# A decoder trunk whose second token half lags one block of rows at each change of sublayer

## The chip, the cores and the metric

The kernel runs on one core of a Trainium2 chip. The metric is the device time of one execution in microseconds, as a median over runs. All matrix work is TensorE's (PE in the profile; PEld is its weight load), ScalarE is ACT, VectorE is DVE, GpSimd is POOL, and SyncE (SP) issues nearly all DMA transfers, in program order.

## The reference, cut to what matters

A trunk of two layers over 256 tokens of width 1024. Layer 0 is FFN, gated short convolution, FFN. Then the keys and values are built once, and layer 1 is FFN, sparse attention, FFN. Every sublayer is wrapped in the same two steps, with shift, scale and gate taken from the condition `c`:

```python
h = modulate_pre(x, g[s, 0], mod[:, s, 0], mod[:, s, 1])   # rms_norm(x) * (1 + scale) + shift
y = sublayer(h)
x = gated_post_add(x, y, g[s, 1], mod[:, s, 2], weight)    # x + weight * gate * rms_norm(y)
...
def swiglu_ffn(h, w_in, w_out):                            # hidden width 2816
    g, u = jnp.split(h @ w_in, 2, axis=-1)
    return (jax.nn.silu(g) * u) @ w_out
```

`mod` is `silu(c) @ ada_w + ada_b`: 18 vectors of 1024, and two more for the keys and values. Attention has 16 heads in 4 groups and three branches (compressed blocks, selected blocks, window), each a masked softmax with linear position penalties, merged by sigmoid gates. With 256 tokens all blocks are selected, so the selected and the window branch are two causal softmaxes with keys and values of their own. All data are float32.

## The kernel before, in words

**Products.** Each float32 product is made of three matmuls in the type fp32r (`mm3`): high part of the activations with high and low part of the weights, low part with high part. The weights are streamed: a DMA brings 1 MB into one of three buffers `raw`, and each half of it, a *unit*, is split into `whi` (ScalarE, a copy that rounds) and `wlo` (VectorE, a subtraction). `fwd(n, g)` splits the next `n` units of a fixed list (`w_init`), and beside them makes `g` adaLN steps. Units lie in two pools, A with room for six and B for four; the list says which. A `raw` buffer takes its next load when both its halves are split (`w_dma`).

**adaLN steps.** One step (`g_step`, line 204) multiplies a 128 x 1024 piece of `ada_w` by the condition and adds along the row, on VectorE. There are 160; 16 are made at the start, the others are strewn among the weight splits by `pump` at the rates `G_FFN`, `G_CONV`, `G_KV` and `G_ATT`. `g_need` makes those still missing when a vector is used.

**Tokens in two halves.** The 256 tokens are two halves of 128 (`t`). An FFN has 11 blocks of 256 hidden columns. For block `b` the kernel makes the input product of half 0 and of half 1 (24 matmuls each), gates and transposes the result to `H[b]`, and adds the rows of the output weights of the block before, `wo(b - 1)`, to the accumulators `y[0]` and `y[1]` (12 matmuls each). All engines' orders are written out by hand.

**A change of sublayer** (`turn_over`) finishes `y[0]`, then `y[1]` with the last two blocks (24 matmuls each), while ScalarE, GpSimd and VectorE take the mean square of `y[0]`, update `x` for half 0, take its mean square and scale it (`normed`). Then TensorE transposes half 0, ScalarE and VectorE modulate and split it into `hx` (`h_split`, lines 354 to 364), and the next sublayer's first product follows. Half 1 goes the same way one step later. The function `first` of the next sublayer gives four pieces of its work, which `turn_over` puts between its own.

**Attention.** `q_first` gives the first query product and the compression: `compress` multiplies 128-row blocks by four unsplit weight pieces `w1` of 1 MB, two for the keys and two for the values, which go through the same `raw` buffers (`w_whole`). `nsa` makes the rest of the queries, the gates (`gates`, weights `bg`) and the compressed keys and values. `heads` is a loop over 16 heads. In iteration `i` it transposes the weights of head `i` (`trans`), scales those of head `i + 1` (`soft_b`, lines 935 to 939), makes minimum and exponential for head `i + 3` (`soft_a`, lines 927 and 928), and issues the scores of head `i + 4`; every second iteration multiplies two heads by the values (`pv`). The compressed branch's scores are turned into exponentials by `cmp_soft` and normalised by the function that it returns (`cmp_norm`, called `fin`), and `cmp_trans` transposes them for `pv`.

**Start.** The condition is loaded into 128 partitions at once and passed through Silu; `x` is normed and transposed; then eight rounds of two adaLN steps, the modulation of one column block and eight matmuls in float32 give the first two blocks of the first FFN.

## Time and profile before

| | |
|---|---|
| median of 3 runs (lowest to highest) | 1077.45 us (1074.9 to 1077.48) |
| the profiled execution: time, span | 1074.75 us, 1073.0 us |
| busy in the span: PE, PEld | 1034.8 us, 829.0 us |
| busy in the span: DVE, ACT, POOL | 776.7 us, 530.5 us, 29.4 us |
| mean granted clock of TensorE | 0.992 of full speed |
| moved by DMA | 263.51 MB, mean 246 GB/s |

Busy time of an engine is the time in which one of its instructions ran. TensorE's matmuls overlap and their ends are modelled, so a busy TensorE need not be at its peak, and the granted clock of a stretch is read beside it. The span runs from the first to the last instruction; 1.75 us of the execution's time lie around it. The profile is of a single execution.

### The profile page before, as it was taken

To read this page: it belongs to the slowest core of one execution; us is meant where nothing else is said; L and a number is where in the kernel's file an instruction comes from. 1 tells how busy PE (TensorE), PEld (TensorE's weight loads), DVE (VectorE), ACT (ScalarE), POOL (GpSimd) and SP (SyncE) were. 2 spreads that over 40 slices of the span, in tenths; PEclk is the share of its full clock that TensorE was granted. 3 is DMA by queue.
4 is the path that set the end of the run, shared out by engine and by line. 5 is a ranking of instruction groups with operands and counts; after the bars stand their busy time and mean duration, and the time that the engine had idled before them with its cause. 6 is when DMAs were issued, how large, how long until landed. Compare 5 with 4: busy or idle time off the path is not lost. (4 is left out here: it accounts for less than half of the span.)

```text
span 1073.0 us, 13377 instructions
## 1 busy us (share of the span) xinstructions
PE 1034.8 (96%) x4862; PEld 829.0 (77%) x4862; DVE 776.7 (72%) x1348; ACT 530.5 (49%) x974; POOL 29.4 (3%) x84
## 2 busy tenths in 40 slices
PE   5999999999999999999999999999989899999997
PEld 3478888878878888887988888886877668888886
DVE  4678878878866788788777787785558675666453
ACT  3344444566555444346664344455378664444342
POOL 0000000010010000001100000001000010000000
PEclk9999999999999999999999999999989999999999
DMA  9978888936836898886647988895411355554541
GB/s 364 415 290 304 324 325 313 354 137 249 301 118 223 301 319 323 324 316 252 233 165 279 341 318 322 310 336 204 189 40 41 119 200 211 197 216 161 196 153 40
DMA packets 51090, 263.51 MB, mean 246 GB/s; under 512 B 5584, under 2 KB 8016, under 8 KB 30288
## 3 DMA queue, kind: packets, MB, share of 16 engines
q1 hardware_dynamic: 50640, 261.61, 66.6%
q0 software_dynamic: 384, 1.05, 0.4%
q8 instruction: 38, 0.62, 0.2%
q14 instruction: 28, 0.23, 0.1%
HBM read 260.54 MB, written 1.05 MB: 244 GB/s over the span
## 5 line engine op out<-in xcount | busy, mean ns | idle before, releaser
L248 PE MATMUL in<-whiA,hx 128*128 128x512 f32 x776 | 305.6, 394 | 3.5 <-ACT hx L355 1.8
L250 PE MATMUL in<-whiA,hx 128*128 128x512 f32 x776 | 304.8, 393 | 0.0
L249 PE MATMUL in<-wloA,hx 128*128 128x512 f32 x776 | 303.3, 391 | 0.8 <-DVE wloA L151 0.8
L151 DVE TENSOR_TENSOR wloA<-raw,whiA 128x1024 fp32r<-128x1024 f32 (+1 forms) x209 | 250.4, 1218 | 48.6 <-ACT whiA L145 48.6
L145 ACT ACTIVATE whiA<-raw 128x1024 fp32r<-128x1024 f32 (+1 forms) x209 | 210.3, 1052 | 13.1 <-DMA raw<-in_wi_dram 4.6
L204 DVE SCALAR_TENSOR_TENSOR graw<-graw,sc 128x1024 f32<-128x1024 f32 x147 | 178.8, 1218 | 0.6 <-DMA graw<-in_ada_dram 0.6
L250 PEld LDWEIGHTS in<-whiA,hx 128*128 128x128 f32 x776 | 146.0, 188 | 35.3 <-DVE hx L358 4.9
L248 PEld LDWEIGHTS in<-whiA,hx 128*128 128x128 f32 x776 | 146.0, 188 | 35.0 <-ACT hx L355 2.8
L418 ACT ACTIVATE sg<-in 128x256 f32<-128x256 f32 x86 | 33.1, 385 | 277.4 <-PE in L250 277.4
L249 PEld LDWEIGHTS in<-wloA,hx 128*128 128x128 f32 x776 | 146.2, 188 | 31.0 <-DVE wloA L151 1.4
L248 PE MATMUL y<-whiB,H 128*128 128x512 f32 x368 | 150.6, 409 | 0.0
L249 PE MATMUL y<-wloB,H 128*128 128x512 f32 x368 | 144.3, 392 | 2.1 <-DVE wloB L151 2.1
L250 PE MATMUL y<-whiB,H 128*128 128x512 f32 x368 | 144.6, 393 | 0.9 <-DVE H L292 0.9
L151 DVE TENSOR_TENSOR wloB<-raw,whiB 128x1024 fp32r<-128x1024 f32 x108 | 129.4, 1221 | 13.8 <-ACT whiB L145 13.8
L419 DVE TENSOR_TENSOR ht<-in,sg 128x256 f32<-128x256 f32 x86 | 36.4, 424 | 115.9 <-ACT sg L418 115.8
L145 ACT ACTIVATE whiB<-raw 128x1024 fp32r<-128x1024 f32 x108 | 108.5, 1054 | 4.6 <-PE in L249 2.8
L250 PEld LDWEIGHTS y<-whiB,H 128*128 128x128 f32 x368 | 69.1, 188 | 16.5 <-DVE H L292 1.6
L249 PEld LDWEIGHTS y<-wloB,H 128*128 128x128 f32 x368 | 69.4, 189 | 15.7 <-DVE wloB L151 3.3
L248 PEld LDWEIGHTS y<-whiB,H 128*128 128x128 f32 x368 | 69.2, 188 | 12.0
L291 ACT ACTIVATE H<-tr 128x256 fp32r<-128x256 f32 x88 | 33.1, 382 | 80.0 <-PE tr L286 80.0
L292 DVE TENSOR_TENSOR H<-tr,H 128x256 fp32r<-128x256 f32 x88 | 36.5, 420 | 28.2 <-ACT H L291 28.2
L286 PE MATMUL tr<-sm,ht 128*128 128x128 f32 x192 | 35.7, 272 | 0.7 <-DVE H L292 0.7
(209 smaller groups left out, 974.9 us busy)
## 6 DMA issues: line engine op xcount, KB each, us to landing
raw<-in_wi_dram SPq DMA_DIRECT2D x84, 1024.0 KB, 6.7
graw<-in_ada_dram SPq DMA_DIRECT2D x147, 512.0 KB, 5.5
raw<-in_wo_dram SPq DMA_DIRECT2D x44, 1024.0 KB, 6.8
raw<-in_cv_dram SPq DMA_DIRECT2D x12, 1024.0 KB, 6.5
whiB<-in_ada_dram SPq DMA_DIRECT2D x8, 512.0 KB, 9.5
raw<-in_ao_dram SPq DMA_DIRECT2D x4, 1024.0 KB, 6.2
raw<-in_q_dram SPq DMA_DIRECT2D x4, 1024.0 KB, 5.4
raw<-in_w_dram SPq DMA_DIRECT2D x4, 1024.0 KB, 7.7
```

The costliest lines, as they stand in the source:

```text
L145: nc.scalar.activation(hi[:, :w], raw, AF.Copy)
L151: nc.vector.tensor_sub(lo, raw, hi.bitcast(F32))
L204: self.nc.vector.scalar_tensor_tensor(w, w, 1.0, self.sc, op0=OP.mult, op1=OP.mult, accum_out=self.mod[:, m, k:k + 1])
L248: mm(out, xh, wh, start=start, stop=False, skip_group_check=True)
L249: mm(out, xh, wl, start=False, stop=False, skip_group_check=True)
L250: mm(out, xl, wh, start=False, stop=stop, skip_group_check=True)
L286: self.nc.tensor.transpose(o[:, i * 128:i * 128 + 128], src[:, i * 128:i * 128 + 128], self.ident)
L291: self.nc.scalar.activation(h[0], src, AF.Copy)
L292: self.nc.vector.tensor_sub(h[1], src, h[0].bitcast(F32))
L418: nc.scalar.activation(sg, o[:, 0:256], AF.Silu)
L419: nc.vector.tensor_mul(ht, o[:, 256:512], sg)
```

## The change

- **Lag.** At the end of an FFN the rows of block 8 are added to `y[0]` in their old place, but to `y[1]` only in the change of sublayer, ahead of blocks 9 and 10 (`late`). After the convolution and attention one row block of eight does the same. The rows of block 10 go to pool A.
- **Rates.** No adaLN steps in the first block of the first FFN and in the last block of each; other rates are changed to match. `turn_over` splits 2 + 2 units in place of 1 + 2, and 2 + 4 in place of 1 + 4 ahead of the keys.
- **Attention.** Three units (the gates' and the first query pair's) are split behind the compression and the second query product, not before them. In the loop the splits of iterations 0, 1, 2 and 12 go, those of 13 and 14 come. The compressed branch's second softmax starts at iteration 5, not 6, and the normalisation stands behind `soft_b` of iterations 1 and 6. Two more units are split before the change to the last FFN.
- **Condition.** `c` is loaded into one partition, two matmuls with a row of ones spread it over 128, and Silu reads the result from PSUM.

```diff
-    G_FFN = (1.5, 1.5, 1.5, 0.45)
-    G_CONV = 0.75
+    G_FFN = (1.65, 1.65, 1.6, 0.45)
+    G_CONV = 1.25
     G_KV = 1.25
-    G_ATT = 1.5
+    G_ATT = 1.0
...
-            p.append((a["wo"][n, b], [("wo", n, b, i) for i in range(2)], "B", 1024))
+            p.append((a["wo"][n, b], [("wo", n, b, i) for i in range(2)], "A" if b == 10 else "B", 1024))
...
-    def turn_over(self, rows, ma, mb, first, mid=None, more=(1, 2)):
+    def turn_over(self, rows, late, ma, mb, first, mid=None, more=(2, 2)):
...
         self.prod_out(0, rows, False, True, each0)
-        self.prod_out(1, rows, False, True, each1)
+        self.prod_out(1, late + rows, False, True, each1)
...
-        g = self.G_FFN[n]
+        rate = self.G_FFN[n]
...
             last = b == 10
+            g = 0 if last or first is not None else rate
...
             if last:
-                self.fwd(3)
-                return nxt(self.rows(n, 9) + self.rows(n, 10), lambda: self.turn_in(h1, H, 1)())
+                self.fwd(2)
+                return nxt(self.rows(n, 9) + self.rows(n, 10), self.rows(n, 8), lambda: self.turn_in(h1, H, 1)())
...
             for i, q in enumerate(wait):
-                self.prod_out(1, self.rows(n, q), new and i == 0, False)
-                Hs.pop(q)
+                if q < 8:
+                    self.prod_out(1, self.rows(n, q), new and i == 0, False)
+                    Hs.pop(q)
...
-        self.prod_out(1, rows(0, 4), True, False)
+        self.prod_out(1, rows(0, 3), True, False)
         self.fwd(2)
-        return nxt(rows(4, 8), None)
+        return nxt(rows(4, 8), rows(3, 4), None)
...
             if i + 1 < NH:
                 soft_b(i + 1)
+            if i in (1, 6):
+                fin()
             if i + 3 < NH:
                 soft_a(i + 3)
...
-            if i in (0, 6):
-                fin = self.cmp_soft(i // 6)
+            if i in (0, 5):
+                fin = self.cmp_soft(i // 5)
             if i + 4 < NH:
                 bias(i + 4)
-            if i in (0, 7):
-                fin()
...
-            if i < 4 or i in (12, 14):
-                self.fwd(1)
+            if i in (3, 13, 14):
+                self.fwd(2 if i == 14 else 1)
...
         o = self.prod(("q0",), 1)
+        self.fwd(3)
         self.then()
...
         self.fwd(4, g)
-        self.prod_out(1, rows(0, 4), True, False)
-        self.fwd(2, 2 * g)
-        return nxt(rows(4, 8), None)
+        self.prod_out(1, rows(0, 3), True, False)
+        self.fwd(4, 2 * g)
+        return nxt(rows(4, 8), rows(3, 4), None)
...
-        nc.sync.dma_start(self.sc, bass.AP(tensor=cc.tensor, offset=cc.offset, ap=[[0, 128], [1, D]]))
+        cr = self.quarter()[0:1, :]
+        nc.sync.dma_start(cr, bass.AP(tensor=cc.tensor, offset=cc.offset, ap=[[0, 1], [1, D]]))
...
-        nc.scalar.activation(self.sc, self.sc, AF.Silu)
+        ones = self.tmp.tile([128, 256], F32, name="sg")[0:1, 0:128]
+        nc.vector.memset(ones, 1.0)
+        for h in range(2):
+            o = self.bank("tr")
+            sl = slice(h * 512, h * 512 + 512)
+            nc.tensor.matmul(o, ones, cr[:, sl], start=True, stop=True)
+            nc.scalar.activation(self.sc[:, sl], o, AF.Silu)
```

VectorE in the first block of the first FFN, before (L151 is the low half of a weight split, L204 an adaLN step, L292 the low half of `H`):

```order
L292 TENSOR_TENSOR H<-tr,H 128x2x128 x4
L151 TENSOR_TENSOR wloA<-raw,whiA 128x1024
L204 SCALAR_TENSOR_TENSOR graw,mod<-graw,sc 128x1024
L151 TENSOR_TENSOR wloA<-raw,whiA 128x1024
L419 TENSOR_TENSOR ht<-in,sg 128x256
L151 TENSOR_TENSOR wloB<-raw,whiB 128x1024
L204 SCALAR_TENSOR_TENSOR graw,mod<-graw,sc 128x1024
L151 TENSOR_TENSOR wloB<-raw,whiB 128x1024 x2
L204 SCALAR_TENSOR_TENSOR graw,mod<-graw,sc 128x1024
```

The same place in the changed kernel:

```order
L292 TENSOR_TENSOR H<-tr,H 128x2x128 x4
L151 TENSOR_TENSOR wloA<-raw,whiA 128x1024 x2
L419 TENSOR_TENSOR ht<-in,sg 128x256
L151 TENSOR_TENSOR wloB<-raw,whiB 128x1024 x4
L419 TENSOR_TENSOR ht<-in,sg 128x256
L292 TENSOR_TENSOR H<-tr,H 128x2x128
L151 TENSOR_TENSOR wloA<-raw,whiA 128x1024
L292 TENSOR_TENSOR H<-tr,H 128x2x128
L151 TENSOR_TENSOR wloA<-raw,whiA 128x1024 x2
L204 SCALAR_TENSOR_TENSOR graw,mod<-graw,sc 128x1024
```

The three adaLN steps that stood between these splits are gone from here; the first step now comes behind nine splits.

SyncE around the compression, before (the 2048-wide loads from `in_w` are the four pieces `w1`; `bg` are the gates' weights):

```order
L130 DMA raw<-in_bg_dram 128x384
L194 DMA graw<-in_ada_dram 128x1024
L130 DMA raw<-in_w_dram 128x2048 x3
L765 DMA cst<-in_cst_dram 128x778
L767 DMA w_6175<-in_w_dram 128x384
L130 DMA raw<-in_w_dram 128x2048
L130 DMA raw<-in_q_dram 128x2048
```

The same place in the changed kernel:

```order
L130 DMA raw<-in_bg_dram 128x384
L130 DMA raw<-in_w_dram 128x2048 x2
L767 DMA cst<-in_cst_dram 128x778
L769 DMA w_6177<-in_w_dram 128x384
L130 DMA raw<-in_w_dram 128x2048 x2
L130 DMA raw<-in_q_dram 128x2048
```

The third piece `w1` has moved from ahead of the constants to behind them, next to the fourth.

VectorE in the first iterations of the loop over heads, before (L856 to L860 are `cmp_soft`, L866 to L873 `fin`, L935 to L939 `soft_b`):

```order
L856 TENSOR_TENSOR small<-cst,in 128x256
L859 TENSOR_REDUCE cm<-small 128x16
L860 TENSOR_TENSOR small<-small,cm 128x256
L866 TENSOR_REDUCE cl<-small 128x16
...
L872 TENSOR_SCALAR cl<-cl,cst 128x8 x2
L873 TENSOR_TENSOR small<-small,cl 128x256
L151 TENSOR_TENSOR wloA<-raw,whiA 128x1024
L935 RECIPROCAL mw<-ml 128x4
L936 TENSOR_TENSOR mw<-mw,G_6178 128x4
L939 TENSOR_SCALAR small<-small,mw 128x128 x2
L939 TENSOR_SCALAR z<-z,mw 128x256 x2
```

The same place in the changed kernel, whose lines stand two further down:

```order
L858 TENSOR_TENSOR small<-cst,in 128x256
L861 TENSOR_REDUCE cm<-small 128x16
L862 TENSOR_TENSOR small<-small,cm 128x256
L937 RECIPROCAL mw<-ml 128x4
L938 TENSOR_TENSOR mw<-mw,G_6180 128x4
L941 TENSOR_SCALAR small<-small,mw 128x128 x2
L941 TENSOR_SCALAR z<-z,mw 128x256 x2
L868 TENSOR_REDUCE cl<-small 128x16
...
L874 TENSOR_SCALAR cl<-cl,cst 128x8 x2
L875 TENSOR_TENSOR small<-small,cl 128x256
```

`soft_b` has moved ahead of the normalisation, and the weight split is gone from here.

## Rows read from the trace of the kernel before

**Rows 1.** The page, busy time of TensorE: us, share, instructions.

```profile
PE 1034.8 (96%) x4862; PEld 829.0 (77%) x4862; DVE 776.7 (72%) x1348; ACT 530.5 (49%) x974; POOL 29.4 (3%) x84
```

**Rows 2.** Waits of TensorE, 71 to 1064 us: total us, times, longest us.

```profile
PE tr L946 <- DVE small L939: 6.4, 2, 3.3
PE in L248 <- ACT hx L355: 2.3, 5, 0.5
PE tr L286 <- ACT T L949: 1.5, 1, 1.5
PE tr L286 <- DVE z L341: 1.5, 4, 0.7
PE in L248 <- ACT whiA L145: 1.2, 1, 1.2
PE y L250 <- DVE H L292: 0.9, 1, 0.9
PE in L249 <- DVE wloA L151: 0.8, 1, 0.8
```

**Rows 3.** Stretches: length, busy PE, PEld, DVE, ACT, POOL; clock; DMA share; GB/s.

```profile
787.60:792.70 5.10, 5.10 (x24) 4.89 (x24) 2.75 (x12) 3.87 (x12) 0.00 (x0) 0.50 0.01 3
839.90:844.50 4.60, 4.53 (x25) 2.82 (x26) 3.35 (x11) 1.91 (x3) 0.00 (x0) 0.63 0.01 2
877.30:882.00 4.70, 3.93 (x10) 2.93 (x11) 4.70 (x5) 4.68 (x6) 0.00 (x0) 0.64 0.27 68
779.60:848.40 68.80, 60.78 (x414) 48.35 (x413) 48.47 (x222) 51.09 (x174) 0.00 (x0) 0.93 0.13 47
```

**Rows 4.** Timeline of the start: start us, us, instruction [idle before it <- releaser].

```profile
0.74 0.40 SPq L1088 DMA_DIRECT2D sc<-in_c_dram  x1
1.20 0.90 SPq L1090 DMA_DIRECT2D x<-in_x_dram  x2
6.18 0.63 ACT L311 ACTIVATE junk<-x 128x512 f32<-128x512 f32 x1 [0.24 <-DMA x<-in_x_dram]
```

**Rows 5.** The page, DMA issues: count, KB each, median us from issue to landing.

```profile
raw<-in_w_dram SPq DMA_DIRECT2D x4, 1024.0 KB, 7.7
...
out_dram<-h SPq DMA_DIRECT2D x4, 256.0 KB, 2.2
sc<-in_c_dram SPq DMA_DIRECT2D x1, 512.0 KB, 4.1
...
raw<-in_bg_dram SPq DMA_DIRECT2D x1, 192.0 KB, 3.8
```

**Rows 6.** Timeline of the first FFN's first block: VectorE and TensorE.

```profile
57.06 1.22 DVE L204 SCALAR_TENSOR_TENSOR graw<-graw,sc 128x1024 f32<-128x1024 f32 x1
...
63.22 0.50 PE L249 MATMUL y<-wloB,H 128*128 128x512 f32 x1 [1.32 <-DVE wloB L151]
```

**Rows 7.** The stretch of the convolution, columns as in rows 3.

```profile
221.00:310.00 89.00, 88.96 (x412) 72.66 (x413) 69.10 (x107) 50.59 (x85) 2.10 (x6) 1.00 0.67 242
```

**Rows 8.** Timeline of TensorE at the first and third change of sublayer.

```profile
216.29 1.07 PE L286 MATMUL tr<-sm,z 128*128 128x128 f32 x8 [0.66 <-DVE z L341]
...
494.22 0.50 PE L250 MATMUL y<-whiB,H 128*128 128x512 f32 x1 [0.92 <-DVE H L292]
```

**Rows 9.** Timeline of the compression, and that load's landing (as rows 5).

```profile
741.74 0.33 SPq L130 DMA_DIRECT2D raw<-in_w_dram  x1
...
746.11 7.12 PE L707 MATMUL in<-raw,quarter 128*60 128x256 f32 x32
...
raw<-in_w_dram SPq DMA_DIRECT2D x1, 1024.0 KB, 4.7
```

**Rows 10.** Timeline of attention's first iterations: VectorE and TensorE.

```profile
781.84 0.42 DVE L860 TENSOR_TENSOR small<-small,cm 128x256 f32<-128x256 f32 x1
...
785.60 1.22 DVE L151 TENSOR_TENSOR wloA<-raw,whiA 128x1024 fp32r<-128x1024 f32 x1
...
787.58 0.45 PE L946 MATMUL tr<-sm,small 128*128 128x128 f32 x1 [3.30 <-DVE small L939]
```

More of the change, by code (lines that the diff above doesn't have):

```diff
@@ L1036, in nsa, with end @@
         self.fwd(4, g)
-        self.prod_out(1, rows(0, 4), True, False)
-        self.fwd(2, 2 * g)
-        return nxt(rows(4, 8), None)
-    def end(self, rows, mid):
+        self.prod_out(1, rows(0, 3), True, False)
+        self.fwd(4, 2 * g)
+        return nxt(rows(4, 8), rows(3, 4), None)
+    def end(self, rows, late, mid):
         nc = self.nc
@@ L1066, in end @@
         self.prod_out(0, rows, False, True, each0)
-        self.prod_out(1, rows, False, True, each1)
+        self.prod_out(1, late + rows, False, True, each1)
         for t in range(2):
@@ L1165, in over @@
         def over(first, ma, mb, **more):
-            return lambda rows, mid: self.turn_over(rows, ma, mb, first(), mid, **more)
+            return lambda rows, late, mid: self.turn_over(rows, late, ma, mb, first(), mid, **more)
         self.ffn(0, 2, over(self.conv_first, 4, 3), first)
@@ L1170, in run @@
         self.ffn_head(1)
-        self.ffn(1, 8, over(self.kv_first, 19, 18, more=(1, 4)))
+        self.ffn(1, 8, over(self.kv_first, 19, 18, more=(2, 4)))
         self.kv_side(self.ffn_first(2))
```

## The prediction

> **What bounds the kernel now.** I read the page's busy times first. TensorE is busy for 1034.8 us of the 1073.0 us span [rows 1], so only its 38 us of idle time, and any time in which it runs slowly, can be won: no instruction of its main work goes away. Next come TensorE's waits between 71 and 1064 us, the part in which it hardly waits [rows 2]. The reader is to see that ten rows there hold 15.8 us, and that 6.4 us are two waits in attention (transposes that wait for a softmax result of VectorE), 1.2 + 0.8 us are weights of the last FFN split too late, 1.5 us are four waits at changes of sublayer, and 0.9 us one more there. The third view is the granted clock by stretch [rows 3]. It falls in three places: to 0.50 right behind the first long wait in attention, 0.63 behind the second and 0.64 behind the late weights; 0.50 is 1.2 GHz, the lower of TensorE's two levels (2.4 is the other). Work at half speed counts as busy, so this loss is hidden in the 1034.8. It is (1 - 0.50) x 5.1 + (1 - 0.63) x 4.6 + (1 - 0.64) x 4.7 = 2.55 + 1.7 + 1.7 = 5.95 us. The first 71 us are read apart: there VectorE's chain of adaLN steps and weight splits paces TensorE.
>
> **The change, part by part.** The sum is made against the profiled execution's 1074.75 us.
>
> *Condition.* The broadcast load of c moves 512 KB and lands after 4.1 us; the two loads of x stand behind it, and the first squares of x start on ScalarE when x is there, at 6.18 us [rows 4, 5]. Everything up to the first matmuls follows from those squares. Now 4 KB are loaded, two matmuls copy them to all partitions, and two Silu from PSUM replace one. Without the 512 KB, x as the first big load would land at 1.20 + 4.1 = 5.3 us: 0.9 us earlier. The other side is the new chain. Its load is issued at 0.74 us; the trace has no 4 KB load, so the nearest rows bound it: 2.2 us to landing for 256 KB on an idle queue at the end, 3.8 us for 192 KB in heavy traffic [rows 5]. Estimating 0.65 us for each matmul and each Silu piece (the fp32 matmuls and 512-wide ACT instructions of this trace are of that size), the last Silu ends at 0.74 + 2.2 + 3 x 0.65 = 4.9 us or at 6.5 us. So the gain is +0.9 us with the first and -0.3 us with the second. The queue is idle at the start, as in the 2.2 us row: I take **+0.9** (-0.3 to 1.2). The Trainium skill, "DMA: Bandwidth & Descriptors", section on the anatomy of one DMA, gives a fixed cost near 2.0 us to which the bytes are added; by it the load lands at 2.8 us and the term stays +0.9. The 3.8 us row speaks against the page, and by that row the term would be -0.3.
>
> *First FFN block without adaLN steps.* A VectorE step takes 1.22 us; three of them stand between weight splits at 57 to 65 us, and TensorE waits for those splits, the longest time 1.32 us [rows 6], twice more 0.4 us, 2.1 us together. With a rate of 0 they go behind this block. I take **+2.1** (0.5 to 2.1; the lower bound if the weight loads are late instead). The steps come back at higher rates, 0.45 a block in the FFNs (0.55 us of VectorE) and 5.5 in the convolution, 6.7 us. The cover is VectorE's idle time: 69.1 of 89 us are busy in the convolution [rows 7]. Without the cover this costs up to 2 us; I take 0.
>
> *The lag.* Twelve matmuls move from block 8's place to the end of the second half, so token half 0 has 12 x 0.23 = 2.8 us more cover for its mean, norm and scaling. TensorE's work is unchanged. What can come back is only what ends in the transposes: 0.66 us at the first change of sublayer [rows 8] and 0.8 us at three others (the 1.5 us row). Another row shows the limit: the first product of each new sublayer waits 2.3 us in all, five times, for ScalarE's split behind those transposes, and the lag does nothing for that wait [rows 2]. At the third change TensorE also waits 0.92 us for the second half of block 10's H [rows 8]; with block 8 first in line this is covered by 1.4 us of matmuls. Some of the 1.5 us is lost again, since ScalarE is still at the last mean when the transposes come earlier: I count 1.1. So 1.1 + 0.9 = **+2.0** (0.9 to 2.4). The price is room: six row units live at once, so block 10's go into pool A. There the next stage's first splits wait until block 10's input weights are used; from then on TensorE has 24 + 36 matmuls, 13.8 us, and the four splits need 4 x 1.05 on ScalarE and 1.22 on VectorE, 5.4 us. Covered.
>
> *The gate weights split later.* They now keep one of three raw buffers through the compression, so its third weight piece is loaded only when the first is used: at 741.74 us, where the fourth is loaded now. That load took 4.7 us, so it lands at 746.4 us; TensorE wants it at 746.11 [rows 9]. That is 0.3 us late, and about 0.3 again for the next piece, whose load then starts one half product later. I take **-0.7**; with the 7.7 us median of all these loads [rows 5] it is 749.4 - 746.1 = -3.3.
>
> *Attention.* In the first iteration VectorE does the compressed branch's normalisation and a 1.22 us weight split ahead of the softmax scaling for which TensorE waits until 787.58 us [rows 10]. In the new order scaling 2 comes directly behind the compressed scores, whose last VectorE step ends at 782.3 us [rows 10]; it takes 1.4 us and is done at 783.7, before the transposes reach it. So the 3.3 us wait goes, and the half clock behind it (2.55 us). In turn the transposed compressed probabilities now want a PSUM bank that ScalarE frees late, by my estimate 1.0 us. Early part: 3.3 + 2.55 - 1.0 = 4.85. In the middle ScalarE is nearly full; the 1.5 us wait for it I leave as it is. At the end a split at iteration 12 delays scaling 14 and TensorE waits 3.1 us, the rest of the 6.4; that split moves behind the scaling, but delays scaling 15 by about 1.5 us. So 3.1 + 1.7 (clock) - 1.5 = 3.3. Together **+8.2** (2 to 12). TensorE's own work remains the largest there: 60.8 of 68.8 us against 51.1 on ScalarE and 48.5 on VectorE, which also lose two splits each [rows 3]. The three splits moved ahead of attention, 3.7 us of VectorE, fall beside the 24 matmuls of q0's second half, behind which both engines only wait for transposes.
>
> *Into the last FFN.* Four units are split, not two, before the change of sublayer: the waits of 1.2 + 0.8 and the slow clock behind them (1.7) go: **+3.7** (0 to 4).
>
> Sum: 0.9 + 2.1 + 2.0 - 0.7 + 8.2 + 3.7 = 16.2 us, so 1058.5 us on the scale of the profiled run. That run lies 2.7 us under the median of 1077.45; halfway I forecast **1059.5 us**.
>
> The clock is 5.95 us of this. The Trainium skill, "TensorE: Matmul & The Clock Gate", section on what is actually happening, says that the lowered clock is the idle state and that activity releases it; by that rule all 5.95 us come back with the waits. The trace agrees so far: each of the three slow stretches stands behind a wait. If instead the thin work in attention caused them, the sum would be 10.3.
>
> **Rivals.**
> *The slow clock stays*, for that reason: 1074.75 - 10.3 = 1064.5 us. Against it: the 1.5 us wait in the same stage is followed by no lower clock. 0.10.
> *ScalarE becomes the bound in attention*: what TensorE gains early it waits for later, and only the two splits taken out of the loop count, 2.1 us, not 8.2: 1064.6 us. For it: the 1.5 us wait in the middle is for ScalarE [rows 2]. Against: over the stage it has 17 us idle [rows 3]. 0.17.
> *The compression waits longer*, 3.3 us, and the clock falls behind it as it does behind the wait of that length in attention (2.55): 16.2 + 0.7 - 5.9 = 11.0, 1063.7 us. 0.08.
> *Little changes*, since other waits take the places of those removed: within 3 us of before. 0.05.
> *Slower*: with pool A full at each of four FFN ends, TensorE waits out the whole 5.4 us of splits: 4 x 5.4 = 21.6 against 16.2, 1080 us. It decides from 4.1 us each. Against it stand the 13.8 us of cover. 0.05.
>
> **How the numbers follow.** The forecast case (a gain of 13 to 22 us) has the remaining 0.55. The range takes in the three middle cases and the bounds of the terms: 1052 to 1069 us. Smaller than 0.3% (3.2 us) no measurement of this kernel tells from no change. Faster 0.90, same 0.05, slower 0.05.
>
> **What would show it.** In the new profile: first squares near 5.3 us; no wait for B splits before 71 us; no 3 us waits for the scaling in attention and a clock of 1.00 there; no late weights after attention; a wait of some tenths in the compression. Attention from its first transposes to the output projection should take about 60 us instead of 68. I am wrong if TensorE's waits there only move, or if a new wait stands at the FFN ends.

## The result, and the profile after

The changed kernel runs in 1063.87 us (median of 5 runs, 1063.58 to 1070.18) against 1077.45 us (5 runs, 1074.9 to 1080.9): ratio 0.9895, 95% interval 0.9858 to 0.9932. Its profiled execution took 1063.87 us with a span of 1062.1; beside the profiled execution of before (1074.75 and 1073.0) it gains 10.9 us. The forecast was 1059.5 us (range 1052 to 1069), from a sum of 16.2 us. So 5.3 us of the sum did not come. (The forecast also slipped by 0.4 us against its own rule: halfway up the 2.7 us from 1058.5 is 1059.9, not 1059.5.)

The page's busy times, to be read beside [rows 1]: TensorE's 1034.8 us have become 1034.4.

```profile
PE 1034.4 (97%) x4866; PEld 826.0 (78%) x4866; DVE 776.7 (73%) x1349; ACT 529.1 (50%) x975; POOL 31.1 (3%) x84
```

That the two totals are nearly the same does not mean that all the gain is idle time. In attention's stretch (below) TensorE's busy time falls by 4.1 us, since work at half clock was counted as busy, and at the start it rises by about as much, since the two new matmuls of the condition are 3.75 us long.

The waits of TensorE in the changed kernel, 71 to 1054 us (line, what it waited for: total us, times, longest us), beside [rows 2]:

```profile
PE in L248 <- ACT hx L355: 3.3, 5, 0.7
PE tr L948 <- ACT T L951: 1.9, 2, 1.1
PE y L248 <- ACT H L291: 1.1, 1, 1.1
PE tr L286 <- ACT T L951: 0.9, 2, 0.6
PE y L250 <- DVE H L292: 0.8, 1, 0.8
PE in L249 <- DVE wloA L151: 0.6, 1, 0.6
...
PE in L709 <- DMA raw<-in_w_dram: 0.3, 1, 0.3
...
PE tr L948 <- DVE small L941: 0.3, 1, 0.3
```

The 6.4 us for the scaling have become 0.3, and the late weights of the last FFN, 1.2 + 0.8, are gone, as are the four waits for `z` and the 0.9 us for `H` at the third change. Three things are new: 1.1 + 0.8 us for `H` at the end of the first FFN, 0.6 us for a weight split, and the wait for the first `hx` has grown from 2.3 to 3.3 us. The granted clock, in the stretches of [rows 3] (columns as there), is 1.00 throughout:

```profile
787.60:792.70 5.10, 4.76 (x37) 3.49 (x36) 3.66 (x20) 4.68 (x18) 0.00 (x0) 1.00 0.00 0
839.90:844.50 4.60, 4.60 (x25) 3.92 (x26) 3.21 (x6) 3.89 (x6) 0.00 (x0) 1.00 0.90 308
780.34:840.40 60.06, 56.72 (x406) 44.42 (x406) 46.04 (x219) 48.14 (x170) 0.00 (x0) 1.00 0.06 19
```

The last row is attention from its first transposes to the output projection: 60.06 us, where the forecast said about 60 in place of 68. Where the gain comes in is seen from the time at which the same instruction starts in each trace, here the first product of each sublayer (the row that waits for `hx`; for the first FFN, whose first two blocks are made at the start, the product of its third block). Two kernels of the experiments stand beside it; the last row of e5 and all rows of e12 from the second on hold falls of the clock.

| first product of | before | changed | e5, no lag | e12, lag alone |
|---|---|---|---|---|
| first FFN | 46.84 | 47.14 | 47.41 | 47.16 |
| convolution | 217.81 | 217.15 | 215.02 | 223.94 |
| second FFN | 314.12 | 314.65 | 312.63 | 320.49 |
| keys and values | 505.64 | 504.85 | 502.96 | 515.38 |
| attention | 731.79 | 731.85 | 730.28 | 743.58 |
| last FFN | 872.36 | 864.93 | 868.77 | 885.87 |

Up to attention, two thirds of the span, the changed kernel has won nothing: 731.85 against 731.79. From the heads' first transposes (779.60, now 780.34) to the last FFN's first product it wins 8.17 us, and from there to the transposes of half 1 (883.97 and 872.74) another 3.8. By stage, the changed kernel gains 1.0 us in the first FFN and 1.3 in the second, and loses 0.3 before the first product, 1.2 in the convolution, 0.9 from the keys and values to attention, 0.7 from there to the heads' transposes and 0.3 at the end; with the 8.2 and 3.8 us above that makes 10.9.

Most of what the first FFN could have won is lost at its end. ScalarE in the changed kernel (start us, duration, instruction, idle before it and releaser):

```profile
193.74 1.06 ACT L145 ACTIVATE whiA<-raw 128x1024 fp32r<-128x1024 f32 x1
198.95 2.01 ACT L145 ACTIVATE whiA<-raw 128x1024 fp32r<-128x1024 f32 x2 [4.16 <-PE in L250]
200.86 0.36 ACT L418 ACTIVATE sg<-in 128x256 f32<-128x256 f32 x1
201.13 0.38 ACT L291 ACTIVATE H<-tr 128x256 fp32r<-128x256 f32 x1
```

and TensorE there:

```profile
198.70 0.38 PE L286 MATMUL tr<-sm,ht 128*128 128x128 f32 x2
201.55 0.50 PE L248 MATMUL y<-whiA,H 128*128 128x512 f32 x1 [1.08 <-ACT H L291]
203.12 0.50 PE L250 MATMUL y<-whiA,H 128*128 128x512 f32 x1 [0.83 <-DVE H L292]
```

Their load's issue on SyncE's timeline, and that issue in the view of DMA issues (the last number is us to landing):

```profile
191.13 0.33 SPq L130 DMA_DIRECT2D raw<-in_cv_dram  x1
```

```profile
raw<-in_cv_dram SPq DMA_DIRECT2D x1, 1024.0 KB, 7.7
```

Two splits of the convolution's weights stand in ScalarE's order ahead of `sg` and `H`. The view puts their wait down to TensorE; their load, 191.13 + 7.7, landed at 198.8, and TensorE had finished block 10 at 198.7. The two are 0.1 us apart, so this trace alone does not say which released them. The trace of e2, which has the same order here, does (ScalarE, then TensorE at the end of block 10):

```profile
198.34 2.01 ACT L145 ACTIVATE whiA<-raw 128x1024 fp32r<-128x1024 f32 x2 [3.47 <-DMA raw<-in_cv_dram]
198.78 0.38 PE L286 MATMUL tr<-sm,ht 128*128 128x128 f32 x2
```

There the splits start on the landing, before TensorE is done with block 10; so it is the load, and not room in pool A. TensorE then waited 1.91 us for `H` behind these splits.

### The profile page after: what moved, and what is told of

It reads as the page before. It is cut to its first block, busy times and chain, and to the rows that moved or that the text cites. A ratio compares the mean times of both kernels' runs of the same rounds, so it can differ in the third digit from the quotient of the medians.

```text
span 1062.1 us, 13417 instructions
## 1 busy us (share of the span) xinstructions
PE 1034.4 (97%) x4866; PEld 826.0 (78%) x4866; DVE 776.7 (73%) x1349; ACT 529.1 (50%) x975; POOL 31.1 (3%) x84
## 4 chain that ended last, share of the span: by engine, by line
PE 84%; DVE 8%; ACT 5%; DMA 2%; issue 1%; POOL 0%; ACTq 0%; DVEq 0%; POOLq 0%
PE in L250 17%; PE in L248 17%; PE in L249 17%; PE y L250 9%; PE y L248 9%; PE y L249 9%; PE tr L286 3%; DVE wloA L151 2%; PE in L709 1%; DVE graw L204 1%; DVE whiB L204 1%; DVE wloB L151 1%; ACT junk L311 1%; DMA raw<-in_cv_dram 1%; ACT z L930 1%
## 5 line engine op out<-in xcount | busy, mean ns | idle before, releaser
L151 DVE TENSOR_TENSOR wloA<-raw,whiA 128x1024 fp32r<-128x1024 f32 x217 | 259.5, 1218 | 44.4 <-ACT whiA L145 44.4
L145 ACT ACTIVATE whiA<-raw 128x1024 fp32r<-128x1024 f32 x217 | 218.6, 1052 | 16.6 <-PE in L250 5.8
L204 DVE SCALAR_TENSOR_TENSOR graw<-graw,sc 128x1024 f32<-128x1024 f32 x147 | 178.8, 1217 | 5.3 <-DMA graw<-in_ada_dram 5.3
L248 PE MATMUL y<-whiB,H 128*128 128x512 f32 x336 | 138.0, 411 | 0.0
L250 PE MATMUL y<-whiB,H 128*128 128x512 f32 x336 | 132.1, 393 | 0.0
L249 PE MATMUL y<-wloB,H 128*128 128x512 f32 x336 | 131.5, 392 | 0.0
L151 DVE TENSOR_TENSOR wloB<-raw,whiB 128x1024 fp32r<-128x1024 f32 x100 | 119.9, 1220 | 11.2 <-ACT whiB L145 11.2
L145 ACT ACTIVATE whiB<-raw 128x1024 fp32r<-128x1024 f32 x100 | 100.0, 1052 | 2.7 <-PE in L249 2.7
L250 PEld LDWEIGHTS y<-whiB,H 128*128 128x128 f32 x336 | 63.0, 188 | 14.1
L249 PEld LDWEIGHTS y<-wloB,H 128*128 128x128 f32 x336 | 63.4, 189 | 11.7 <-DVE wloB L151 0.2
L248 PEld LDWEIGHTS y<-whiB,H 128*128 128x128 f32 x336 | 63.2, 188 | 11.0
L292 DVE TENSOR_TENSOR H<-tr,H 128x256 fp32r<-128x256 f32 x88 | 36.5, 420 | 28.8 <-ACT H L291 28.8
L327 DVE TENSOR_TENSOR z<-y,g 128x512 f32<-128x512 f32 x24 | 16.6, 690 | 33.3 <-ACT junk L311 29.8
```

The source lines that it names most:

```text
L145: nc.scalar.activation(hi[:, :w], raw, AF.Copy)
L151: nc.vector.tensor_sub(lo, raw, hi.bitcast(F32))
L204: self.nc.vector.scalar_tensor_tensor(w, w, 1.0, self.sc, op0=OP.mult, op1=OP.mult, accum_out=self.mod[:, m, k:k + 1])
L248: mm(out, xh, wh, start=start, stop=False, skip_group_check=True)
L249: mm(out, xh, wl, start=False, stop=False, skip_group_check=True)
L250: mm(out, xl, wh, start=False, stop=stop, skip_group_check=True)
```

## The experiments

Each kernel ran beside the kernel before. Since the granted clock falls in some executions of a kernel and not in others (below), times are compared between executions without such a fall, and the profile is read ahead of it.

### Attention: e1 and e2

e1: the kernel before with the new loop order alone.

```diff
+        self.fwd(2)                       # nsa, behind the second query product
+            if i in (1, 6):
+                fin()                     # behind soft_b(i + 1)
-            if i in (0, 7):
-                fin()
-            if i in (0, 6):
-                fin = self.cmp_soft(i // 6)
+            if i in (0, 5):
+                fin = self.cmp_soft(i // 5)
-            if i < 4 or i in (12, 14):
-                self.fwd(1)
+            if i in (3, 13, 14):
+                self.fwd(2 if i == 14 else 1)
```

> The kernel before with the new order of the loop over heads alone (scaling ahead of the normalisation, splits of iterations 3, 13 and 14), two units split behind the second query product, everything else as before. Theory (the two 3 us waits and the slow clock behind them are the attention gain, whatever stands around): the two waits for the scaling go, the clock is 1.00 in the loop, about 8.0 us less than the kernel before, some 1066.7 us on the scale of its profiled run; the late weights of the last FFN and the waits at the changes of sublayer stay as before. Rival (the gain needs the other parts, for instance the lag or the later gate weights): less than 4 us.

Measured: 1067.35 us (4 runs, lowest 1067.13), ratio 0.9916 (0.9886 to 0.9947). From attention's first product (731.86 us) to the last FFN's (864.41) it takes 132.55 us, the kernel before 140.57: 8.0 us less, and the clock is 1.00 in the loop. The late weights remain (1.2 + 0.8). So the attention term needs no other part of the change.

e2: the changed kernel with the first wait put back.

```diff
-            if i in (1, 6):
+            if i == 6:
                 fin()
...
                 fin = self.cmp_soft(i // 5)
+                if i == 0:
+                    fin()
-            if i in (3, 13, 14):
+            if i in (0, 13, 14):
```

> The changed kernel with the normalisation and a weight split ahead of the scaling again in iteration 0, as before, and nothing else. Theory (the wait makes the low clock): TensorE waits about 3 us for the scaling, the granted clock falls to about 0.5 for some 5 us behind it, and the time is about 5 us longer, 1069 us. Rival (the low clock in attention had another cause, such as the state of the engine at that time of the program): the wait of 3 us comes back, the clock stays at 1.00, and the time is about 3 us longer, 1067 us.

Measured: 1067.92 to 1068.13 us in three runs, 4.3 us over the changed kernel's three at 1063.58 to 1063.87; the fourth, 1073.63, is the profiled one and has a further fall of the clock near 770 us. TensorE's timeline, and the stretch behind the wait (the clock is the third number from the end):

```profile
794.03 0.45 PE L948 MATMUL tr<-sm,small 128*128 128x128 f32 x1 [3.28 <-DVE small L941]
```

```profile
794.00:800.00 6.00, 5.97 (x31) 5.78 (x32) 5.44 (x31) 2.92 (x11) 0.00 (x0) 0.57 0.02 4
```

The wait costs 3.28 us and the clock (1 - 0.57) x 6.0 = 2.6. Of these 5.9 us 4.3 show in the time: later waits for ScalarE's `T` are 1.1 us shorter (1.7 in place of 2.8), and 0.5 us stay unaccounted for. A single wait put back brings its slow clock with it: the theory holds, the rival does not.

### The start: e3

```diff
-            nc.scalar.activation(self.sc[:, sl], o, AF.Silu)      # ahead of the squares
+        for h in range(2):                                        # behind the four squares
+            nc.scalar.activation(self.sc[:, h * 512:h * 512 + 512], cb[h], AF.Silu)
```

> The changed kernel with the two Silu pieces of the condition behind the four squares of x on ScalarE, not ahead of them. Theory (the start loses because the squares stand behind Silu, which waits for two slow float32 matmuls, while x has landed near 5.3 us): first squares at about 5.3 us instead of 6.53, everything up to the first FFN block about 1.2 us earlier, and the time 0.5 to 1.2 us shorter, about 1062.8 us. Rival (the first adaLN step needs the Silu and then starts later, or x itself lands no earlier than 6 us): no gain, 1063.9 us.

In the changed kernel the new chain looks like this (TensorE, then ScalarE):

```profile
2.25 3.75 PE L1123 MATMUL tr<-quarter,sg 1*128 1x512 f32 x4 [2.25 <-DMA quarter<-in_c_dram]
```

```profile
4.33 0.60 ACT L1124 ACTIVATE sc<-tr 128x512 f32<-128x512 f32 x1 [2.31 <-PE tr L1123]
6.03 0.60 ACT L1124 ACTIVATE sc<-tr 128x512 f32<-128x512 f32 x1 [1.11 <-PE tr L1123]
6.53 0.62 ACT L311 ACTIVATE junk<-x 128x512 f32<-128x512 f32 x1
```

The 4 KB landed 1.5 us after their issue, faster than either bound, but the two matmuls took 3.75 us, not 1.3. The Trainium skill, "DMA: Bandwidth & Descriptors", section Anatomy of one DMA, from which the prediction has its 2.0 us, speaks there of DMAs that GpSimd issues; this one is SyncE's, and the landing was faster. The squares, behind the two Silu in ScalarE's order, begin at 6.53 us; in e3 they begin with the landing of `x`:

```profile
5.20 0.63 ACT L311 ACTIVATE junk<-x 128x512 f32<-128x512 f32 x1 [3.19 <-DMA x<-in_x_dram]
```

The first FFN's first product starts at 46.55 us (47.14 in the changed kernel, 46.84 before). This time differs between executions of the same start: 46.81 to 47.16 in before, e1 and e12, 47.14 to 47.42 in the changed kernel, e2, e4, e5 and e6, 46.43 to 46.58 in e3, e7 to e10, but 47.47 in e11. The median, 1067.14 us, shows nothing of it: the profiled execution has two falls of the clock. By the profile the theory holds with 0.6 us, half of what was hoped; the time is inconclusive. The Trainium skill, "FP8 and Floating Point Precision", section TensorE Precision Notes, says that true float32 makes four passes through the array. The trace shows two rows for each of the two matmuls, 0.94 us a row; four passes no run here shows.

### What the lag and the first block are worth: e4, e5, e6, e12

e4: at the end of the first FFN alone, `H` ahead of the splits.

```diff
-            self.fwd(3 if last else 2 * len(wait), g)
+            if not (last and n == 0):
+                self.fwd(3 if last else 2 * len(wait), g)
             h1 = self.evac_in(o)
             H = Hs[b] = self.H_tile()
             self.turn_in(h0, H, 0)()
+            if last and n == 0:
+                self.fwd(3)
```

> The changed kernel with the gating of block 10 and its rows H of token half 0 ahead of the three weight splits at the end of the first FFN alone, not behind them. Theory (these splits wait until 198.9 us for a weight load that lands late, and H stands behind them on ScalarE and VectorE, so TensorE waits 1.1 + 0.8 us): both waits go, and the time is 1.5 to 1.9 us shorter, about 1062.2 us. Rival (pool A is full and the splits wait for TensorE, so that they only shift and the next wait takes the gain): 1063.9 us, with a new wait of 1 to 2 us for a split or for H of half 1.

Measured: both waits go, one of 0.42 us for a low half comes, and the convolution's first product starts at 215.69 us, 1.46 earlier, though the start was 0.28 later. At attention's first product 1.62 us are left. The profiled execution then loses 4.7 us to a fall of the clock; the median is 1067.25 us, the lowest run 1063.06, 0.5 under the changed kernel's. The cause of the wait is shown; of the 1.7 us the whole times show only 0.5.

e5: the changed kernel without the lag (block 8 and row block 3 in their old places, block 10's rows in pool B).

```diff
-                if q < 8:
-                    self.prod_out(1, self.rows(n, q), new and i == 0, False)
-                    Hs.pop(q)
+                self.prod_out(1, self.rows(n, q), new and i == 0, False)
+                Hs.pop(q)
...
-                return nxt(self.rows(n, 9) + self.rows(n, 10), self.rows(n, 8), ...)
+                return nxt(self.rows(n, 9) + self.rows(n, 10), [], ...)
```

> The changed kernel without the lag: block 8's rows (and the row block 3 after the convolution and attention) are added for half 1 in their old place, and block 10's rows go to pool B again. Theory (what the lag wins it gives back: the waits for z and H, 2.4 us, go, but ScalarE's split of the first hx is 0.2 us later five times, and TensorE reaches the end of the first FFN 2.8 us earlier than its weight load, which costs 1.9 us there): the z waits return, 1.5 us, and the H wait at the third change, 0.7 to 0.9 us, the 1.9 us at the first FFN's end go, the hx waits fall from 3.3 to 2.3 us; the sum is between -0.8 and +0.5 us, about 1063.5 us where the clock stays up. Rival (the prediction's term stands): 2.0 us longer, 1065.8 us.

Its waits, 71 to 1059 us:

```profile
PE in L248 <- ACT hx L355: 2.3, 5, 0.5
...
PE tr L286 <- DVE z L341: 1.1, 4, 0.3
...
PE in L708 <- DMA raw<-in_w_dram: 0.6, 2, 0.4
```

No wait for `H` is left at any change of sublayer, those for `hx` are back at 2.3 us, and `z` costs 1.1. The load lands at 198.1 us (198.8 in the changed kernel), but now it is in time, since TensorE ends block 10 at 201.65, 3 us later than with the lag:

```profile
198.14 2.01 ACT L145 ACTIVATE whiA<-raw 128x1024 fp32r<-128x1024 f32 x2 [0.41 <-DMA raw<-in_cv_dram]
201.85 0.38 ACT L418 ACTIVATE sg<-in 128x256 f32<-128x256 f32 x1 [1.70 <-PE in L250]
```

Attention's first product starts at 730.28 us, 1.57 before the changed kernel's though e5 started 0.27 later. So the lag costs 1.8 us there, where the prediction gave it +2.0 (and the expectation up to 0.8). The rival falls. e4, which keeps the lag but puts `H` ahead of the splits, is there at 730.23 us after the same start, so what the lag loses is this one queue.

The whole times do not show it. e5's median is 1067.30 us (lowest 1064.16), over the changed kernel's, with a fall of the clock in all four runs (mean clock 0.994 or 0.995). So the 1.8 us are read from traces up to attention, and whether leaving out the lag makes the fall more frequent stays open.

e6: the changed kernel with adaLN steps in the first block again.

```diff
-            g = 0 if last or first is not None else rate
+            g = 0 if last else rate
```

> The changed kernel with adaLN steps in the first block of the first FFN again, at the new rate. Theory (what is won there is lost at the end of that FFN, where a weight load paces the end): the waits for the low halves of the B splits return at 60 to 67 us, about 2.1 us, the wait for H near 201 us shrinks by 1.5 us or more, and from the first change of sublayer on the two kernels run within 0.5 us of each other; 1064 us. Rival (the late load has another cause and does not move with TensorE): both waits stand, and the time is 2 us longer, 1066 us.

```profile
62.51 0.50 PE L249 MATMUL y<-wloB,H 128*128 128x512 f32 x1 [1.54 <-DVE wloB L151]
63.65 0.50 PE L249 MATMUL y<-wloB,H 128*128 128x512 f32 x1 [0.17 <-DVE wloB L151]
67.06 0.50 PE L249 MATMUL y<-wloB,H 128*128 128x512 f32 x1 [0.40 <-DVE wloB L151]
```

The 2.1 us are back, but the wait for `H` near 204 us shrinks only from 1.91 to 1.25, and the convolution starts 2.34 us later (219.49), 0.09 of it from the start. Lowest of nine runs 1066.84, 3.3 us over; median 1071.45. My theory, that the end of the FFN gives this gain back, falls: the first block's gain is real and stays. The rival's number is the nearer one, but not its reason: the load did move with TensorE (issued at 194.16 us, 3.0 later), which is why the wait for `H` hardly shrank.

e12: the kernel before with the lag alone. Three units before the change of sublayer do not fit into pool A beside block 10's rows, so it has 2 + 2 in place of 3 + 1, as the change has.

```diff
-            p.append((a["wo"][n, b], [...], "B", 1024))
+            p.append((a["wo"][n, b], [...], "A" if b == 10 else "B", 1024))
...
-        self.prod_out(1, rows, False, True, each1)
+        self.prod_out(1, late + rows, False, True, each1)
...
-                self.fwd(3)
+                self.fwd(2)
...
+                if q < 8:
```

> The kernel before with the lag alone (block 8's rows late, block 10's rows in pool A, 2 + 2 units split around the changes of sublayer, since 3 + 1 would not fit in pool A). The prediction's term: 2.0 us less than the kernel before, the waits for z (1.5 us) and for H at the third change (0.9 us) gone, 0.4 us lost at the first hx. Theory after e5_no_lag: z and H gain 2.4 us, hx loses 1.0 us, and at the end of the first FFN TensorE comes 2.8 us earlier to H, which stands behind splits that wait for a load, and waits 1 to 1.9 us there; the sum is between -0.5 and +0.4 us.

Measured: 1090.36 us (4 runs, lowest 1086.75), ratio 1.0134 (1.0105 to 1.0163): 14 us slower than before. Its first FFN's end, ScalarE, VectorE and TensorE:

```profile
202.13 2.01 ACT L145 ACTIVATE whiA<-raw 128x1024 fp32r<-128x1024 f32 x2 [4.31 <-PE tr L286]
204.31 0.37 ACT L291 ACTIVATE H<-tr 128x256 fp32r<-128x256 f32 x1
204.37 1.22 DVE L204 SCALAR_TENSOR_TENSOR graw<-graw,sc 128x1024 f32<-128x1024 f32 x1
205.51 1.22 DVE L151 TENSOR_TENSOR wloA<-raw,whiA 128x1024 fp32r<-128x1024 f32 x1
206.98 0.41 DVE L292 TENSOR_TENSOR H<-tr,H 128x256 fp32r<-128x256 f32 x1
207.45 0.80 PE L250 MATMUL y<-whiA,H 128*128 128x512 f32 x1 [1.98 <-DVE H L292]
```

The load (issued at 194.16, 7.9 us) lands at 202.1; behind it stand two splits and, on VectorE, an adaLN step, which this kernel still makes in the last block, and then `H`. TensorE waits 1.23 + 1.98 us, and the clock is 0.60 from 205 to 210 us and 0.71 for the next five. At the ends of the second and third FFN `H` costs 0.33 + 2.38 and 0.94 us. Both numbers expected are wrong by far. The mechanism is the one that e5 showed, at three ends in place of one (at the second the view itself names the load: the splits start at 494.20 us, before TensorE ends block 10 at 494.70), with the old steps behind it in the same queue; what the lag and what the 2 + 2 splits cost apart from these steps, this run does not separate.

### Mended versions: e7, e9, e10

e7 is the changed kernel with e3's and e4's edits, the gate weights split before the compression again, and a lower rate in the convolution.

```diff
-    G_CONV = 1.25
+    G_CONV = 1.0
...
-        self.ffn(2, 11, over(self.q_first, 13, 12, more=(0, 0)))
+        self.ffn(2, 11, over(self.q_first, 13, 12, more=(0, 1)))
...
         o = self.prod(("q0",), 1)
-        self.fwd(3)
+        self.fwd(2)
```

> The changed kernel with four places mended: squares ahead of Silu at the start, H of block 10 ahead of the splits at the first FFN's end, the gate weights split before the compression again, and a lower rate of adaLN steps in the convolution (1.0 for 1.25). By the profile: 0.6 + 1.7 + 0.3 to 0.6 + 0.6 us less, about 3 us, 1060.7 us where the clock stays up. Rival (each removed wait comes back at the next load, since the loads pace the first three sublayers): 1062.5 us or more.

Measured: 1068.05 us, lowest 1065.22. The first end is mended (convolution at 214.62 us), and the compression waits for no load. But the convolution, with the lower rate, waits more (1.04 and 0.43 us in place of 0.63), and `H` is late at the two other ends, where the changed kernel's profile had no such wait: 0.78 + 0.84 us and 0.65 + 0.83, with a clock of 0.64 behind the last. The rival holds.

e9 joins the diffs of e5 (no lag), of e3 (squares first) and the last two pieces of e7's (gate weights early).

> The changed kernel without the lag, with the squares ahead of Silu at the start and the gate weights split before the compression. Theory (the lag loses some 1.6 us by the profile of e5_no_lag, the late squares 0.6 to 1.0 us, the late w1 piece 0.3 to 0.6 us): TensorE reaches the first product of attention at about 729.5 us instead of 731.85, there is no wait for a load in the compression and none for H at an end of an FFN, and the time without a fall of the clock is 1060.8 us, 1064.5 with one near 766 us. Rival (what is won is lost at the next loads): 1063.5 us at best.

Measured: 1065.6 us, two of six runs at 1060.87 and 1060.93, the fastest of all. Its first product of attention starts at 729.37 us:

```profile
729.37 0.50 PE L248 MATMUL in<-whiA,hx 128*128 128x512 f32 x1 [0.45 <-ACT hx L355]
```

The compression waits for no load, and no end of an FFN for `H`. That is the expected 1060.8 where the clock stays up; in four of six runs it does not.

e10 keeps the lag: the diff of e3, those two pieces of e7's, and e4's edit at three ends.

```diff
-            if not (last and n == 0):
+            if not (last and n < 3):
```

> The changed kernel with the lag, the squares ahead of Silu, the gate weights split before the compression, and H of block 10 ahead of the weight splits at the ends of the first three FFNs. Theory (the lag itself is worth a little; its loss is H standing behind splits that wait for a load): no wait for H at any of the three ends, first product of attention at about 729.5 us, and 1060.8 us without a fall of the clock. Rival (the late splits then delay the means or the next first product): waits of 0.5 us or more for a split behind the changes of sublayer, 1062 us.

Measured: 1063.62 us (5 runs, 1062.44 to 1064.77), ratio 0.9878 (0.9862 to 0.9894). No wait for `H`, but 0.42 us for a low half at each of the three ends and 0.5 us for another at 151 us; attention starts at 731.71. The rival holds: the late splits take the gain. By the trace e9, without the lag, is 2.3 us ahead at attention; by the medians e10 is 2.0 us ahead, since the clock fell in four of e9's six runs.

### The fall of the clock near 766 us: e8 and e11

Six profiles (e2 to e6, e9) show a clock of 0.50 from 766 to 773 us on, those of before, of the changed kernel, of e1, e7, e10 and e12 do not. Some show another fall elsewhere: e3 at 203 us, e7 at 720, e8 at 816, e9 at 805. e8 is e7, and e11 is e9, with dense work moved there.

```diff
         gates()
+        self.q_half(2, 0)
         self.cmp_values()
...
         self.cmp_scores(0)
-        self.q_half(2, 0)
```

> The kernel e7_mended with one more edit: the first half of the third query product (24 matmuls) stands ahead of the compressed values, not behind the compressed scores. In three of four profiles of the last experiments the granted clock fell to 0.50 near 766 us for some 10 us and cost about 4.6 us, in others not. Theory (the thin work and the two waits of 0.4 us between 760 and 767 us make the clock fall): with dense work in between the clock stays at 1.00 there in all executions, the wait for the compressed values' operand goes (0.4 us), and the longest runs are no more than 1 us above the shortest: 1060.3 us. Rival (the fall has nothing to do with these waits): the spread of 4 to 5 us between executions stays as it is, and the shortest time is that of e7_mended.

> The kernel e9_no_lag_mended with the first half of the third query product ahead of the compressed values. Theory (dense work between the thin pieces shortens the fall of the clock near 766 us, as in e8_mended_thick, where it cost some 1.7 us in place of 4.6): median 1 to 3 us under that of e9_no_lag_mended, longest run no more than 3 us above the shortest. Rival (chance from one execution to the next): the same median and spread as e9_no_lag_mended.

e8 measured 1067.66 us (1065.6 to 1068.57): 7 us over what was expected, the clock did fall (0.65 over 776 to 780 us), and its lowest run is no better than e7's, as its rival says; only the spread is smaller. e11 measured 1063.83 (1063.04 to 1064.37), 1.8 under e9. The same place in e4 and in e11:

```profile
766.20:776.60 10.40, 10.40 (x49) 9.84 (x48) 7.28 (x27) 5.63 (x21) 0.00 (x0) 0.51 0.51 192
```

```profile
766.00:772.00 6.00, 6.00 (x47) 5.54 (x46) 4.87 (x14) 2.54 (x9) 0.00 (x0) 1.00 0.06 7
772.00:779.00 7.00, 7.00 (x32) 6.58 (x30) 4.79 (x30) 3.10 (x14) 0.00 (x0) 0.52 0.39 144
```

The fall comes later and is shorter, and the spread narrows to 1.3 us. But e11's four runs all have a mean clock of 0.994 or 0.995, so it seems to fall in each, where e9 escapes in two of six. e11's numbers came as its theory said, and the theory holds for the length of the fall, not for whether the clock falls. Four and six runs do not settle it.

## Why the prediction was right and where it failed

**Attention, right.** +8.2 was forecast; 8.17 came, and e1 alone gives 8.0. The first part of the loop gives 5.0 of the 4.85 forecast (18.05 us from the first transposes at 780.34 to those at 798.39, 23.08 before, from 779.60 to 802.68). The waits for ScalarE's copies `T` are now 2.8 us where 1.5 were (the rival that ScalarE becomes the bound came true by 1.3 us). That the sum agrees so closely is partly luck: of the two losses taken off, 1.0 for the bank came as 0.34 and 1.5 for scaling 15 as 0.28, and in their place stand those 1.3 us and 0.6 us more between the output projection and the last FFN (24.5 for 24.0 us). The clock's share came back in full: it is 1.00 where the wait is gone, and e2 shows wait and slow clock (0.57) together, so the rival of a slow clock that stays falls. The Trainium skill's rule ("TensorE: Matmul & The Clock Gate", section What's actually happening) that activity releases the lowered clock agrees with these stretches.

**Into the last FFN, right.** +3.7 forecast, 3.8 measured.

**First FFN block, right.** +2.1 forecast: the waits are gone, and e6 puts the price at 2.3 us.

**The lag, wrong in sign.** The failed step: "So 1.1 + 0.9 = **+2.0** (0.9 to 2.4)", with its price "Covered". By e5 it is -1.8 up to attention. The 0.9 us for `H` at the third change did not need the lag (e5 has no such wait). The prediction has this wait covered by block 8's matmuls, but in the trace it stands in `y[0]`, ahead of the place where the lag puts them. VectorE in the kernel before, ahead of the matmul at 494.22 us:

```profile
490.73 1.22 DVE L204 SCALAR_TENSOR_TENSOR graw<-graw,sc 128x1024 f32<-128x1024 f32 x1
493.75 0.42 DVE L292 TENSOR_TENSOR H<-tr,H 128x256 fp32r<-128x256 f32 x1
```

An adaLN step of the last block stood ahead of `H`, and the new rates take it away. With the old rates the wait is there without the lag (e1, 0.67 us) and with it (e12, 2.38). The waits for `z` are worth 1.1 in e5, and against them stand 1.0 us at five first `hx`, for which the prediction has the lag do nothing, and 1.91 us at the end of the first FFN. I asked whether the four splits have room in pool A, and found 13.8 us of cover. I did not ask when the load that they wait for lands, and what stands behind them: `H`, for which TensorE comes earlier by those 12 matmuls. The slower rival had the right place (splits at an FFN's end that TensorE must wait out) with another cause, and at one end of four in the changed kernel. With the old rates and steps in the last block, in e12, it is three ends and a kernel slower than before.

**Condition, wrong.** "Estimating 0.65 us for each matmul": two took 3.75 us. The trace of before had the number, but 0.6 to 0.7 us is one of its rows, and a float32 matmul is two rows: the code issues four a round at the start (not eight, as said above), and a round has eight rows. The first four rows took about as long as the condition's four, later ones half of it, at a granted clock of 1.00 in both stretches; why, no run shows:

```profile
14.76 3.58 PE L1143 MATMUL in<-raw,h 128*128 128x512 f32 x4 [1.88 <-ACT hx L1139]
18.18 1.88 PE L1143 MATMUL tr<-raw,h 128*128 128x512 f32 x4
```

+0.9 became -0.3 (first squares 6.53 for 6.18 us), no more than the start differs between executions. `x` lands at 5.2 us as estimated, but ScalarE is not free to use it; e3 gets 0.6 us of it.

**Gate weights, right in mechanism.** "That is 0.3 us late": the wait is 0.34 us. The second 0.3 did not come.

**Higher rates, wrong.** "Without the cover this costs up to 2 us; I take 0": VectorE's idle time in the stage as a whole is no cover at the place where a split is wanted. In the changed kernel a step stands between two splits, and TensorE waits for the second (VectorE, TensorE):

```profile
267.99 1.21 DVE L204 SCALAR_TENSOR_TENSOR graw<-graw,sc 128x1024 f32<-128x1024 f32 x1
269.14 1.22 DVE L151 TENSOR_TENSOR wloA<-raw,whiA 128x1024 fp32r<-128x1024 f32 x1
270.41 0.50 PE L249 MATMUL in<-wloA,hx 128*128 128x512 f32 x1 [0.63 <-DVE wloA L151]
```

Before, the two splits follow each other without a step:

```profile
267.12 2.35 DVE L151 TENSOR_TENSOR wloA<-raw,whiA 128x1024 fp32r<-128x1024 f32 x2
```

From the convolution's first product to the second FFN's it is 96.3 to 96.6 us at the old rate (before, e1, e12) and 97.5 to 97.9 at the new one (the changed kernel, e2 to e6, e9 to e11): 1.2 us, of which this wait is 0.63. A rate of 1.0 did not mend it (e7, 98.2). Against it stand the 0.9 us that the rates won at the third change.

Measured, the terms are -0.3 + 2.1 - 1.8 - 1.2 + 0.9 - 0.3 + 8.2 + 3.8 = 11.4, against 10.9 us between the profiles; 0.5 us stay unaccounted for. Of the missing 5.3 us the lag is 3.8, the condition 1.2.

## What to carry to other kernels

Where an in-order engine waits for a load, all that stands behind it in its order waits too: before work is moved so that the fastest engine arrives earlier, look up when the load lands and what is queued behind the instruction that needs it. Ask of every wait that a change removes which other edit would remove it as well, or the same 0.9 us is paid for twice. Idle time of an engine over a stage is no cover at one place in its order. The gain that rested on the clock came here where the slow stretch followed a wait that went away.

## What was not expected of the hardware

The granted clock fell near 766 us in some executions and not in others of the same kernel: the changed kernel's five runs have mean clocks of 0.998 to 0.999 (1063.58 to 1063.87 us) and of 0.993 and 0.991 (1068.23 and 1070.18). In e4 it costs 4.7 us (28.33 us from the compressed values at 764.05 to the wait at 792.38, where the changed kernel needs 23.6). TensorE waits at most 0.42 us at a time in the 15 us before; what runs there is thin (products 48 columns wide, transposes of 60). So a long wait is not the only thing behind which the clock falls; why a busy TensorE loses its clock here in one execution and keeps it in another, no run settles. Executions of one kernel differ by some 5 us for it, and medians with them; whether an edit changes how often the clock falls stays open.
